# Keeping split mixer weights in DRAM between the two segments of a hybrid decoder block

## The chip, the cores and the metric

One core of a Trainium2 chip runs the whole program. The metric is the device time of one execution in microseconds (us), as the median of several runs. TensorE (PE) does the matrix products, VectorE (DVE) and ScalarE (ACT) the element-wise work, GpSimd (POOL) small copies, and SyncE (SP) issues nearly all DMA transfers. A transfer is spread over up to 16 DMA engines, whichever engine issued it.

## The reference

Input is a sequence of 1024 tokens of width 1024, to which 16 learned meta tokens are prepended (1040 in all). One layer is computed:

```python
h = h + 0.5 * swiglu(rmsnorm(h, ffn1_norm), ffn1_w_gu, ffn1_w_down)      # D_FF 2816
u = rmsnorm(h, mix_norm)
aq, ak, av, az, abeta, aalpha, bcols, ga, gb = split(u @ w_in)           # one input projection
o_a = deltanet(aq, ak, av, az, ...)      # chunked gated DeltaNet, 8 heads of 128
o_b = rwkv7(bcols, ...)                  # RWKV-7 time mixing, 16 heads of 64
h = h + (sigmoid(ga) * o_a + sigmoid(gb) * o_b) @ w_out
h = h + 0.5 * swiglu(rmsnorm(h, ffn2_norm), ffn2_w_gu, ffn2_w_down)
return rmsnorm(h, final_norm)[:, 16:]
```

All arrays are float32, and w_in has, with padding, 75 column tiles of 128.

## The kernel before, in words

The program has three parts one after the other: `ffn1`, `middle` (the two mixers) and `ffn2`. Activations lie transposed, with the model dimension on the 128 partitions and tokens along the free axis.

**Products in two parts.** To keep float32 accuracy at a fast rate of TensorE, every operand of a large product is split into a rounded high part and a low remainder (`split`: ACT writes the high part on L163, DVE the remainder on L164), and three products hi·hi, hi·lo, lo·hi are summed (`mm3`, L307). A weight tile `w` of the mixers therefore has the shape 128 x 2 x 8 x 128: 4 KB per partition for each of the two parts, 1 MB in all, made from a raw tile `wraw` of 512 KB.

**Two segments.** The sequence goes through the mixers in two segments of 528 and 512 tokens (`SEGS`), since the recurrences carry state from one to the other. Each segment needs all 75 column tiles of w_in, so the kernel loads and splits each tile twice: 75 tiles in the first segment, the same 75, in the same roles, in the second. After those come 16 tiles of w_out.

**The order of the weights.** `weight_order` lists every weight tile in the order of its use. `loadw`, called just before a tile's products (in `proj`, whose matmuls write the PSUM tile `pp`), first calls `fetchw` for tiles ahead of the one in use: one tile ahead (`AHEAD = 1`) for w_in. `fetchw` takes a `wraw` tile (two buffers), issues the load from SP's queue (L260), takes a `w` tile (two buffers, `WB = 2`) and splits the one into the other. A buffer comes free when the last instruction that touches it is done.

**The order of the work.** The heads are done in 8 steps per segment. `schedule` says in which order the actions of neighbouring steps are written down: `new_b` and `new_a` project three column tiles each and prepare the operands of a later step, `gates` projects three more, `operands`, `inverses`, `merge_blocks`, `transitions` and `chains` do the recurrences, and `finish` writes one head's result. What is written down earlier has the higher priority; the tool that builds the program orders each engine's instructions by it, taking what it expects to be ready, so the projections' matmuls fill places between the small matmuls of the recurrences. At run time each engine then works strictly in its own fixed order.

**The chain of the inverses.** In each step DVE inverts small triangular blocks (`inverses`: `tb` on L1627, `Xb` on L1629, the copy `Yt` on L1630). The results go through DRAM to be laid out anew, all from SP's queue: `scX` (L1632, twice) and `scY` (L1634, twice) are written, `Xc` (L1637) and `Y` (L1641, four times) are read back. In the first segment `scY` has 51 rows for each of its two transfers, in the second 48. POOL copies a part of `Xc` to `XA` (L1643), and TensorE's first matmul of `merge_blocks` (`iv<-Xc`, L1662) needs `Xc`. Before the inverses, `scr` (L1594, L1597) and `Ub` (L1603) take the blocks to the layout that DVE works on.

**POOL in the mixers.** It does short copies and memsets: `carB` and `carA` (state that the second segment needs), the first columns of `xr` and of the shifted tiles, `XA`, `gam`, `egl`. It issues DMA transfers only at the borders of `middle` (`rdr`, `h2dr`, `h3dr`).

Of the kernel before, what the change touches and what calls it, by code (L numbers as in the profile page):

```python
# [8 lines left out]
F32 = mybir.dt.float32  # L9
F32R = mybir.dt.float32r  # L10
# [3 lines left out]
P = 128  # L14
D = 1024
KD = D // P
# [22 lines left out]
WB = 2  # L39
AHEAD = 1  # L40
# [70 lines left out]
def build(tc, nc, a):  # L111

    ctx = ExitStack()
    with ctx:
        g = K()
        g.tc, g.nc, g.a = tc, nc, a
        nc.scalar.preload_act_table_set("natural_log_exp_and_others")
        pad = ctx.enter_context(tc.tile_pool(name="pad", bufs=1, side="right"))
        nc.vector.memset(pad.tile([P, 24], F32, name="pad"), 0.0)
        const = ctx.enter_context(tc.tile_pool(name="const", bufs=1))  # L120
        wp = ctx.enter_context(tc.tile_pool(name="wp", bufs=2))
        dram = ctx.enter_context(tc.tile_pool(name="dram", bufs=1, space=bass.MemoryType.DRAM))
        g.mmctx = ctx.enter_context(ExitStack())
        main_banks(g, 2, 3, 8)
        g.const, g.wp, g.dram = const, wp, dram

        ones = const.tile([P, P], F32, name="ones")
        nc.vector.memset(ones, 1.0)
        g.pk = const.tile([P, NPK], F32, name="pk")
        nc.sync.dma_start(g.pk, a["pk"])  # L130

        def pv(n):
            o, w = PK[n]
            return g.pk[:, o : o + w]

        nc.vector.tensor_scalar(pv("omu"), pv("mu"), -1.0, 1.0, op0=ALU.mult, op1=ALU.add)
        nc.vector.tensor_scalar(pv("oka"), pv("ka"), -1.0, 1.0, op0=ALU.mult, op1=ALU.add)
        for n in ("w0", "a0"):
            nc.vector.tensor_scalar(pv(n), pv(n), -1.0, None, op0=ALU.mult)
        g.C = lambda n: ones if n == "ones" else g.ck[:, CK[n][0] - P : CK[n][0] - P + CK[n][1]]  # L140
        g.V = lambda n, i=0: g.pk[:, PK[n][0] + i : PK[n][0] + i + 1]

        hdr = [dram.tile([KD, P, sn], F32, name=f"hdr{s}") for s, (_, sn, _) in enumerate(SEGS)]
        mdr = [dram.tile([NJ, P, FULL], F32, name=f"mdr{s}") for s in range(2)]
        g.hdr, g.mdr = hdr, mdr
        g.sdr = dram.tile([NJ, P, P + CB], F32, name="sdr")
        g.gdr = [dram.tile([NJ, FULL], F32, name=f"gdr{s}") for s in range(2)]
        g.rdr = dram.tile([P, FULL], F32, name="rdr")
        g.h2dr = dram.tile([KD, P, FULL], F32, name="h2dr")
        g.h3dr = dram.tile([KD, P, FULL], F32, name="h3dr")  # L150
        g.frm = dram.tile([len(FORMS), HF, P, T // 2], F32, name="frm")

        g.worder, g.wready, g.wfetched, g.wused = list(weight_order()), [], 0, 0
        ffn1(g)
        middle(g)
        ffn2(g)


def split(g, src, hi, lo, eng=None, hi_eng=None):
    if hi_eng:  # L160
        hi_eng.tensor_copy(hi, src)
    else:
        g.nc.scalar.activation(hi, src, AF.Copy)  # L163
    (eng or g.nc.vector).tensor_tensor(lo, src, hi.bitcast(F32), op=ALU.subtract)  # L164
# [6 lines left out]
def schedule():  # L171

    last = 2 * NJ - 1
    yield "segment", 0
    for act in FIRST.split():
        yield act.rstrip("+"), act.count("+")
    for it in range(last + 1):
        order = {NJ - 2: BEFORE_SWITCH, NJ - 1: SWITCH, last - 1: LAST_BUT_ONE, last: FINAL}.get(it, REGULAR)
        for act in order.split():
            if act == "segment":  # L180
                yield act, 1
            else:
                yield act.rstrip("+"), it + act.count("+")
# [11 lines left out]
def weight_order():  # L195

    def down_order(n):
        for r in range(len(FORMS)):
            for m in range(HK):
                for k0, kk in CHUNKS:  # L200
                    yield f"wdn{n}", (r, m, k0), kk

    def tiles(cts, j=0):
        for ct in cts:
            yield "win", (ct + j % NJ,), KD

    yield from down_order(1)
    for act, it in schedule():
        yield from tiles(USES.get(act, ()), 0 if act == "segment" else it)
    for _ in range(2):  # L210
        for m in range(KD):
            yield "wout", (m,), KD

    yield None
    yield from down_order(2)
# [14 lines left out]
def down_weights(g, name, raw, r, m, k0, kk):  # L230

    s = g.wsum[:, m, k0 : k0 + kk]
    if r == 4 and k0 == 0:
        in_turn(g, g.wsum[:, m], block(g, name, m, 0, 0))
    if raw is None:
        return s
    i, j = ((1, 0), (0, 0), (0, 1), None, (1, 0), (0, 1))[r - 1]
    in_turn(g, raw, block(g, name, m, i, j, k0, kk))
    if r == LAST:
        return raw  # L240
    x, y = (raw, s) if r == 3 else (s, raw)
    g.nc.gpsimd.tensor_tensor(s, x, y, op=ALU.add if r == 1 else ALU.subtract)  # L242
    return s


def fetchw(g):
    if not g.worder[g.wfetched]:
        del g.worder[g.wfetched]
    name, idx, kk = g.worder[g.wfetched]
    g.wfetched += 1  # L250
    down = name.startswith("wdn")
    raw = None
    if not down or idx[0] not in (0, 4):
        raw = g.wp.tile([P, KD, P], F32, name="wraw", tag="wraw", bufs=2)[:, :kk]
    if down:
        src = down_weights(g, name, raw, *idx, kk)
        g.wcount += 1
    else:
        src = raw
        g.nc.sync.dma_start(raw, g.a[name][idx])  # L260
    if down and idx[0] == LAST and g.held:
        w = g.held.pop(0)
    elif down and g.wcount % 3 == 0:
        w = g.wthird.tile([P, 2, CHUNKS[0][1], P], F32R, name="w3", tag="w3", bufs=1)
    else:
        w = g.wp.tile([P, 2, KD, P], F32R, name="w", tag="w", bufs=WB)
    split(g, src, w[:, 0, :kk, :], w[:, 1, :kk, :])
    g.wready.append((name, idx, w))


def loadw(g, name, *idx):

    while g.wfetched < len(g.worder) and g.worder[g.wfetched]:
        down = g.worder[g.wfetched][0].startswith("wdn")
        if g.wfetched > g.wused + AHEAD + down or (name == "wdn1" and not down):
            break
        fetchw(g)
    g.wused += 1
    n, i, w = g.wready.pop(0)
    assert (n, i) == (name, idx)  # L280
    return w


def main_banks(g, w, n, banks=6):

    g.mmctx.close()
    g.mmw = w
    pool = lambda name, bufs: g.mmctx.enter_context(
        g.tc.tile_pool(name=name, bufs=bufs, space=bass.MemoryType.PSUM, reuse_waits="tile"))
    g.mm = pool("mm", n)  # L290
    g.mx = pool("mx", banks - n * w)
# [19 lines left out]
class Rms:  # L311


    def __init__(self, g, sq, n, add_on=None):
        self.g, self.sq, self.n, self.acc, self.k = g, sq, n, None, 0
        self.eng = add_on or g.nc.vector
# [331 lines left out]
class Hidden:  # L648
# [15 lines left out]
    def ahead(self):  # L664
        g = self.g
        g.wcount, g.turn, g.held, g.direct = 0, None, [], self.direct
        sums = lambda m: g.nc.sync.dma_start(g.wsum[:, m], block(g, self.name, m, 1, 1))
        self.even += self.places("11", "21")
        self.slots = self.even[:]
        self.load(8, 0)  # L670
        yield
        yield
        sums(0)
        fetchw(g)
        self.split(3)
        yield
        self.even += self.places("t2")
        self.slots = self.even[:HF]
        self.load(HF, 0)
        self.split(6)  # L680
        yield
        sums(1)
        self.split(8)
        yield
        fetchw(g)
        self.split(HF - 1)
        for m in (2, 3):
            sums(m)
        yield
# [31 lines left out]
def down(g, hs, which, n, hidden, hooks):  # L721
# [20 lines left out]
    for r in range(len(FORMS)):  # L742
        cols = halves(n)
        kept = {}
        for m in range(HK):
            hidden.step(r, m)

            def w(k0):
                kept[m, k0] = loadw(g, f"wdn{which}", r, m, k0)
                if k0:  # L750
                    hooks.before(r, m)
                return kept[m, k0]

            product(r, m, (w, w), cols[-1:] if r == LAST else cols)
            hooks.after(r, m, 0)
        if r == LAST and len(cols) > 1:
            for m in range(HK):
                w = lambda k0: kept[m, k0]
                product(r, m, (w, w), cols[:1])
                if m < 2:  # L760
                    fetchw(g)
                hooks.after(r, m, 1)
# [1202 lines left out]
```

## Time and profile before

| | |
|---|---|
| median of 3 runs | 2983.96 us (2981.35 to 2986.49) |
| the profiled execution: its time / its span | 2987.61 us / 2985.8 us |
| mean granted clock of TensorE | 0.990 of full speed |
| first segment of the mixers, projections (about) | 701 to 1480 us |
| second segment, projections (about) | 1480 to 2212 us |
| output projection (about) | 2212 to 2310 us |

The span runs from the first to the last instruction. In rows of the profile, `pp<-uk,w` reads as "writes pp, reads uk and w", `x75` is a count, and what stands in brackets or behind `<-` is the idle time of the engine before the instruction and what ended it. A row by windows gives start and end, the length, then for PE, PEld (TensorE's weight load), DVE, ACT and POOL the busy us and the count, the granted clock, the share of the 16 DMA engines' time and GB/s.

### The profile page before, as it was taken

Reading aid. Unit: us, or ns where it says so; the run is one execution under the profiler, and the core shown is the slowest. Engines: PE = TensorE matmul, PEld = TensorE weight load, DVE = VectorE, ACT = ScalarE, POOL = GpSimd, SP = SyncE. Lnnn points to the kernel's source line nnn. Section 1 sums busy time; section 2 is a strip of 40 time slices with the busy share of each in tenths; the row PEclk is TensorE's granted clock in tenths of the full one; section 3 lists DMA queues with packets and bytes.
Section 4 is the critical chain, followed back from the end, with each engine's and each line's share of the span. In section 5 each row is a group of like instructions: output and inputs, shape, how many; then the busy total and the mean of one; then the engine's idle time right before and its main releaser. Section 6 shows DMA issues by size and latency. Waiting matters only on the chain.

```text
span 2985.8 us, 62816 instructions
## 1 busy us (share of the span) xinstructions
PE 2879.7 (96%) x25584; PEld 2492.5 (83%) x25584; DVE 2209.0 (74%) x4108; ACT 1452.7 (49%) x2554; POOL 498.4 (17%) x576
## 2 busy tenths in 40 slices
PE   8999999999899999999998999999999999999998
PEld 8999999998878888888776777777777888888786
DVE  8666668776767877788877887778876766667886
ACT  6322234345555656565566556656644422223444
POOL 0333233323000000000000000001001032222421
PEclk9999999999989999999999999999999999999999
DMA  3323236553222222333232332233344332333662
GB/s 134 127 105 107 102 121 206 178 195 115 71 69 71 81 71 68 84 81 85 91 96 72 79 85 71 75 88 83 111 138 177 131 107 104 105 104 130 234 220 100
DMA packets 285601, 333.60 MB, mean 112 GB/s; under 512 B 172448, under 2 KB 178720, under 8 KB 285312
## 3 DMA queue, kind: packets, MB, share of 16 engines
q1 hardware_dynamic: 281872, 320.40, 34.5%
q0 software_dynamic: 2000, 6.56, 0.6%
q8 instruction: 201, 3.29, 0.5%
q10 hardware_dynamic: 1440, 2.63, 0.2%
q14 instruction: 88, 0.72, 0.1%
HBM read 261.86 MB, written 67.64 MB: 110 GB/s over the span
## 4 chain that ended last, share of the span: by engine, by line
PE 67%; DVE 19%; ACT 6%; DMA 4%; issue 3%; SPq 1%; POOL 0%; DVEq 0%; ACTq 0%; POOLq 0%
PE pg L513 24%; PE pp L307 16%; PE pd L733 8%; DVE w L164 3%; PE pwo L307 2%; DVE form L164 2%; PE pg L537 1%; DMA form<-frm 1%; DVE tb L1627 1%; DVE Xb L1629 1%; ACT w L163 1%; PE vp L1312 1%; PE mp L1312 1%; PE xp L1312 1%; PE cs L1259 1%
## 5 line engine op out<-in xcount | busy, mean ns | idle before, releaser
L307 PE MATMUL pp<-uk,w 128*128 128x512 f32 (+2 forms) x4824 | 969.6, 347 | 13.5 <-DVE w L164 5.9
L307 PEld LDWEIGHTS pp<-uk,w 128*128 128x128 f32 x4824 | 744.5, 191 | 111.5 <-DVE w L164 14.8
L733 PE MATMUL pd<-form,w 128*128 128x256 f32 (+2 forms) x2772 | 438.6, 320 | 11.1 <-DVE w L164 9.2
L733 PEld LDWEIGHTS pd<-form,w 128*128 128x128 f32 x2772 | 398.1, 190 | 51.1 <-DVE w L164 12.2
L513 PE MATMUL pg<-bt,w 128*128 128x256 f32 (+2 forms) x2520 | 401.7, 318 | 2.5 <-DVE w L164 2.5
L513 PEld LDWEIGHTS pg<-bt,w 128*128 128x128 f32 x2520 | 360.3, 188 | 36.4 <-DVE w L164 3.8
L164 DVE TENSOR_TENSOR w<-wraw,w 128x1024 fp32r<-128x1024 f32 (+2 forms) x266 | 348.4, 1310 | 47.8 <-ACT w L163 45.8
L519 DVE TENSOR_TENSOR c<-c,pg 128x520 f32<-128x520 f32 (+1 forms) x280 | 189.5, 689 | 240.2 <-PE pg L513 216.0
L163 ACT ACTIVATE w<-wraw 128x1024 fp32r<-128x1024 f32 (+2 forms) x266 | 276.3, 1040 | 177.1 <-PE pg L513 115.9
L513 PE MATMUL pg<-b,w 128*128 128x256 f32 (+2 forms) x2160 | 348.1, 317 | 0.0
L513 PEld LDWEIGHTS pg<-b,w 128*128 128x128 f32 x2160 | 309.9, 188 | 28.3 <-DVE w L164 0.3
L163 ACT ACTIVATE w<-wrx 128x1024 fp32r<-128x1024 f32 (+1 forms) x64 | 58.4, 912 | 278.7 <-PE pg L513 239.9
L483 POOL TENSOR_TENSOR wrx<-wrx 128x512 f32<-128x512 f32 x38 | 52.5, 1381 | 612.1 <-DVE w22b L164 435.6
L164 DVE TENSOR_TENSOR form<-form 128x520 fp32r<-128x520 f32 (+1 forms) x152 | 142.2, 971 | 16.2 <-ACT form L163 15.8
L163 ACT ACTIVATE w<-wsum 128x768 fp32r<-128x768 f32 x96 | 75.7, 788 | 156.2 <-PE pd L733 123.1
L164 DVE TENSOR_TENSOR w<-wsum,w 128x768 fp32r<-128x768 f32 x96 | 119.7, 1253 | 34.9 <-ACT w L163 34.9
L163 ACT ACTIVATE form<-form 128x520 fp32r<-128x520 f32 (+1 forms) x152 | 94.2, 632 | 84.4 <-DMA form<-frm 78.5
L1629 DVE TENSOR_TENSOR Xb<-Xb,tb 115x126 f32<-115x126 f32 (+22 forms) x496 | 126.0, 254 | 8.7
L1627 DVE TENSOR_TENSOR tb<-Ub,Xb 115x126 f32<-115x126 f32 (+22 forms) x496 | 125.1, 252 | 8.8 <-DMA Ub<-scr 1.3
L242 POOL TENSOR_TENSOR wsum<-wsum,wraw 128x768 f32<-128x768 f32 (+1 forms) x48 | 94.8, 1988 | 212.4 <-DMA wraw<-in_wdn 211.0
L1436 DVE SCALAR_TENSOR_TENSOR acc<-xr,pk,acc 128x528 f32<-128x528 f32 (+1 forms) x144 | 109.2, 758 | 20.6 <-ACT acc L1432 19.8
L307 PE MATMUL pwo<-uk,w 128*128 128x512 f32 x384 | 96.6, 401 | 1.1 <-DVE uk L164 0.7
(439 smaller groups left out, 4405.0 us busy)
## 6 DMA issues: line engine op xcount, KB each, us to landing
wraw<-in_win SPq DMA_DIRECT2D x150, 512.0 KB
wraw<-in_wgu SPq DMA_DIRECT2D x44, 512.0 KB
wrx<-in_wgu SPq DMA_DIRECT2D x44, 512.0 KB
frm<-c SPq DMA_DIRECT2D x76, 260.0 KB
form<-frm SPq DMA_DIRECT2D x76, 260.0 KB
frm<-c SPq DMA_DIRECT2D x76, 256.0 KB
form<-frm SPq DMA_DIRECT2D x76, 256.0 KB
wraw<-in_wdn SPq DMA_DIRECT2D x40, 384.0 KB
```

Source lines behind the costliest of these rows:

```text
L163: g.nc.scalar.activation(hi, src, AF.Copy)
L164: (eng or g.nc.vector).tensor_tensor(lo, src, hi.bitcast(F32), op=ALU.subtract)
L242: g.nc.gpsimd.tensor_tensor(s, x, y, op=ALU.add if r == 1 else ALU.subtract)
L307: g.last_product = g.nc.tensor.matmul(ps, lhsT=l, rhs=r, start=i == 0, stop=i == n - 1)
L483: sums.tensor_tensor(a22, a21, a22, op=ALU.add)
L513: nc.tensor.matmul(ps[:, c0 : c0 + cn], lhsT=l[:, x, k, :], rhs=r[:, k, y, c0 : c0 + cn], start=i == 0, stop=i == 3 * HK - 1)
L519: nc.vector.tensor_tensor(o, x, y, op=ALU.add)
L733: nc.tensor.matmul(pd[:, c0 : c0 + cn], lhsT=wd[:, u, k - k0, :], rhs=x[:, v, c0 : c0 + cn], start=k + i == 0, stop=k == HF - 1 and i == 2)
L1312: g.nc.tensor.matmul(ps[e][HS[dst], c0 : c0 + CB], lhsT=l, rhs=r, start=True, stop=True)
L1436: nc.vector.scalar_tensor_tensor(acc[:, :n], xr[:, tap : tap + n], V("convw", ct * 4 + tap), acc[:, :n], op0=ALU.mult, op1=ALU.add)
L1627: nc.vector.tensor_tensor(tv, U[:, i, i + 1 :].unsqueeze(2).to_broadcast([npt, nt, ncc]), X[:, i, 0:ncc].unsqueeze(1).to_broadcast([npt, n ...
L1629: nc.vector.tensor_tensor(X[:, i + 1 :, 0:ncc], X[:, i + 1 :, 0:ncc], tv, op=ALU.add)
```

## The change

In the first segment, a tile of w_in that has been split is also written to DRAM as it stands (`wkept`, 1 MB each, 75 of them, in all 78.6 MB), from POOL's queue. `keep` is called in `fetchw` with a lag: the store of a tile is written down when the tile two further on is fetched. In the second segment `fetch_kept` reads the two parts back from SP's queue straight into the place of `w`, without a `wraw` tile and without a split. Since `wraw` isn't needed there, every third tile goes into its two buffers (`Pair`: two loads of 512 KB), so there are three places instead of two, and the fetch runs two tiles ahead instead of one. The test for that looks at the tile's index alone, so it also holds for the w_out tiles with the indices 0 to 7.

```diff
+        g.wkept = [dram.tile([P, 2, KD, P], F32, name=f"wkept{i}") for i in range(75)]
+        g.kept, g.unkept = set(), []
...
+class Pair:
+    def __init__(self, *parts):
+        self.parts = parts
+    def __getitem__(self, at):
+        p, x, k, c = at
+        return self.parts[x][p, k, c]
+
+def keep(g):
+    idx, w = g.unkept.pop(0)
+    g.nc.gpsimd.dma_start(g.wkept[idx[0]], w.bitcast(F32))
+    g.kept.add(idx)
+
+def fetch_kept(g, name, idx):
+    src = g.wkept[idx[0]]
+    g.wcount += 1
+    if g.wcount % 3:
+        w = g.wp.tile([P, 2, KD, P], F32R, name="w", tag="w", bufs=WB)
+        g.nc.sync.dma_start(w.bitcast(F32), src)
+    else:
+        w = Pair(*(g.wp.tile([P, KD, P], F32R, name="wpart", tag="wraw", bufs=2) for _ in range(2)))
+        for x in range(2):
+            g.nc.sync.dma_start(w.parts[x].bitcast(F32), src[:, x])
+    g.wready.append((name, idx, w))
...
 def fetchw(g):
...
     down = name.startswith("wdn")
+    if name == "win" and len(g.unkept) > (idx not in g.kept):
+        keep(g)
+    if idx in g.kept and name == "win":
+        return fetch_kept(g, name, idx)
...
     split(g, src, w[:, 0, :kk, :], w[:, 1, :kk, :])
+    if name == "win":
+        g.unkept.append((idx, w))
     g.wready.append((name, idx, w))
...
 def loadw(g, name, *idx):
...
-        if g.wfetched > g.wused + AHEAD + down or (name == "wdn1" and not down):
+        if g.wfetched > g.wused + AHEAD + (down or g.worder[g.wfetched][1] in g.kept) or (name == "wdn1" and not down):
             break
         fetchw(g)
```

## The prediction

> **What bounds the kernel now.** I read the page's head and its busy times first, then a row for each stage by windows, then what TensorE waited for in the second segment, then the stretches where it waited.
>
> ```profile
> span 2985.8 us, 62816 instructions
> PE 2879.7 (96%) x25584; PEld 2492.5 (83%) x25584; DVE 2209.0 (74%) x4108; ACT 1452.7 (49%) x2554; POOL 498.4 (17%) x576
> ```
>
> ```profile
> 200.00:300.00 100.00, 100.00 (x839) 100.00 (x838) 58.89 (x72) 28.49 (x37) 31.70 (x22) 1.00 0.27 94
> 701.00:1480.00 779.00, 741.77 (x8665) 639.04 (x8663) 583.99 (x1423) 456.09 (x917) 58.29 (x194) 0.98 0.28 77
> 1480.00:2212.00 732.00, 700.98 (x7646) 558.68 (x7647) 585.23 (x1373) 450.85 (x852) 60.04 (x125) 0.99 0.32 85
> 2212.00:2310.00 98.00, 95.02 (x779) 74.67 (x778) 61.41 (x109) 42.33 (x73) 11.48 (x22) 0.98 0.59 193
> ```
>
> TensorE is the bound in every stage. In the second segment, where work is removed, it is busy 700.98 of 732.00 us, so 31.0 us is all the idle time there; DVE, from which most is taken, is busy 80%. Whatever DVE is relieved of, only the part of those 31.0 us that hangs on DVE or ACT can come back, and the time that a low clock costs. Who ended TensorE's waits there:
>
> ```profile
> PE bon L1259 <- ACT hl L163: 9.7, 7, 1.8
> PE pp L307 <- DVE w L164: 4.3, 2, 2.8
> PE np L1312 <- DVE AR L1738: 4.1, 6, 0.8
> PE pp L307 <- ACT acc L1432: 3.0, 1, 3.0
> ```
>
> Three of the longest stand together at 1605 us:
>
> ```profile
> 1605.92 0.73 PE L307 MATMUL pp<-uk,w 128*128 128x512 f32 x2 [2.96 <-ACT acc L1432]
> 1608.21 1.69 PE L1259 MATMUL bon<-hl,bdr 128*128 128x512 f32 x2 [1.56 <-ACT hl L163]
> 1612.73 1.65 PE L307 MATMUL pp<-uk,w 128*128 128x512 f32 x3 [2.82 <-DVE w L164]
> ...
> 1589.84 1.22 DVE L164 TENSOR_TENSOR w<-wraw,w 128x1024 fp32r<-128x1024 f32 x1
> 1611.45 1.22 DVE L164 TENSOR_TENSOR w<-wraw,w 128x1024 fp32r<-128x1024 f32 x1
> ...
> 1604.00:1608.00 4.00, 0.73 (x2) 0.30 (x2) 4.00 (x11) 3.43 (x6) 1.12 (x3) 0.92 0.00 0
> 1608.00:1612.00 4.00, 1.59 (x2) 0.58 (x2) 4.00 (x11) 0.62 (x2) 0.00 (x0) 0.50 0.00 0
> 1612.00:1616.00 4.00, 3.27 (x8) 2.60 (x9) 4.00 (x9) 2.58 (x5) 0.00 (x0) 0.50 0.41 131
> 1616.00:1620.00 4.00, 4.00 (x16) 3.17 (x15) 2.06 (x5) 0.11 (x1) 0.00 (x0) 0.80 0.74 160
> ```
>
> There DVE is busy without a gap (4.00 of 4.00 us in three rows), TensorE waits 7.34 us in all, and its clock is then granted at half: 0.64 + 4 + 4 + 1.6 = 10.2 us at half, in which it is busy about 6.5 us (1.59 + 3.27 + 1.6), work of 3.2 us at full clock. So the three waits cost 7.3 + 3.2 us.
>
> **What is removed: 75 loads of 512 KB and 75 splits in the second segment.** All splits of the mixers' tiles in this window:
>
> ```profile
> L164 DVE TENSOR_TENSOR w<-wraw,w 128x1024 fp32r<-128x1024 f32 x77 | 94.5, 1227 | 5.6 <-ACT w L163 5.1
> L163 ACT ACTIVATE w<-wraw 128x1024 fp32r<-128x1024 f32 x75 | 79.0, 1054 | 2.8 <-PE pp L307 2.5
> ```
>
> 75 x 1.227 = 92 us leave DVE and 79 us leave ACT; DVE falls from 80% to 67% of the window. Nearly all of it lay beside TensorE's work. What returns, by place. At 1605: the wait of 2.82 us for a split goes; of the other 4.52 us the two DVE splits in the busy stretch before them (2 x 1.22 = 2.4 us) go; the low clock goes with it, 3.2 us. That is 8.4 us. Elsewhere the wait for w is 4.3 - 2.8 = 1.5 us, all of it. The waits for `bon` are 9.7 - 1.56 = 8.1 us in six places; ACT's `hl` comes behind DVE's chain of `new_b`, in which splits are mixed: I take half, 4.0 us (bounds 0 and 8.1). The waits for `np` end with one DVE instruction behind others: a third of 4.1, 1.4 us. The gain is 8.4 + 1.5 + 4.0 + 1.4 = 15.3 us. Its bounds: 4.3 us (the waits for w alone) and 31.0 + 3.2 = 34 us.
>
> **What is added in the second segment: loads of 1 MB from SP's queue.** Their price in engine time: the first stage moves large rows at 94 GB/s in 0.27 of the engines' time, 348 GB/s at full use, so 1 MB takes 3.0 us and 512 KB 1.5 us. Landing, by the nearest row of a large transfer:
>
> ```profile
> L930 POOL DMA_DIRECT2D h3dr<-hh x8: 539/540/544, 2285.9 to 2327.0; - x8
> DMA to landing us min/median/max: 2.3/2.4/9.1
> ...
> 1480.13 21.67 PE pp L307 x94
> ```
>
> 256 KB from POOL's queue land in 2.4 us; 768 KB more at 348 GB/s add 2.3, so 4.7 us is the lower bound, and four times 2.4 = 9.6 us the upper; I take 4.7, since these rows move large packets too. With three places, a tile's load starts when TensorE is done with the tile three before it, and two tiles lie between: 24 matmuls x 21.67 / 94 = 5.5 us each, 11.1 us. Both bounds fit: nothing, while cover lasts; without it 5 us at each run of six projections. SP now waits for TensorE at these loads instead of for DVE; behind it stand the transfers of the inverses' chain, which are needed later than the tile waited for. The 25 further issues of the pairs lie on SP, which ends none of the four waits above. The one tile more of prefetch at w_out: nothing, at most the 3.0 us idle of its window.
>
> **What is added in the first segment: 75 stores of 1 MB from POOL.** Issue: 0.54 us each by the row above, 2.2 us if it grew with size; 41 to 162 us on an engine that is busy 58.29 of 779 us. I take nothing. The store waits for DVE's remainder; queued behind it on POOL are `carB`, `carA`, `XA` and `gam`, and TensorE waits for `XA` alone; the upper end is 2.2 us in each of 8 steps, 18 us.
>
> The store also holds the `w` place: the split of the tile two further on must wait until it has landed. The tightest regular place:
>
> ```profile
> 1007.40 1.22 DVE L164 TENSOR_TENSOR w<-wraw,w 128x1024 fp32r<-128x1024 f32 x1
> ...
> 1016.42 1.06 ACT L163 ACTIVATE w<-wraw 128x1024 fp32r<-128x1024 f32 x1
> ```
>
> The first ends a tile at 1008.62, the second begins the next tile in the same place: 7.8 us of room for 0.54 + 4.7 = 5.2 us. Nothing; at the upper landing 10.1 us it is 2.3 us late, once in each of 8 steps, 18 us.
>
> **Where I see the cost: the inverses' chain.** 75 x 3.0 us more put the engines' share from 0.28 to 0.57 in this segment, and two stores fall on each step's chain:
>
> ```profile
> 1017.64 1.22 DVE L164 TENSOR_TENSOR w<-wraw,w 128x1024 fp32r<-128x1024 f32 x1
> 1024.86 1.22 DVE L164 TENSOR_TENSOR w<-wraw,w 128x1024 fp32r<-128x1024 f32 x1
> ...
> 1019.79 2.45 SPq L1632 DMA_DIRECT2D scX<-Xb  x2
> 1026.67 2.98 SPq L1637 DMA_DIRECT2D Xc<-scX  x1
> ...
> 1032.53 1.39 POOL L1643 COPY XA<-Xc 32x128 f32<-32x128 f32 x2 [3.13 <-DMA Xc<-scX]
> 1034.24 0.75 PE L1662 MATMUL iv<-Xc,LT 32*32 32x32 f32 x32
> ...
> 1408.53 2.01 POOL L1643 COPY XA<-Xc 32x128 f32<-32x128 f32 x2 [2.51 <-DMA Xc<-scX]
> 1410.86 0.75 PE L1662 MATMUL iv<-Xc,LT 32*32 32x32 f32 x32
> ...
> 851.80 0.75 PE L1662 MATMUL iv<-Xc,LT 32*32 32x32 f32 x32 [1.33 <-DMA Xc<-scX]
> ...
> 1785.34 0.97 POOL L1643 COPY XA<-Xc 32x128 f32<-32x128 f32 x2 [1.42 <-DMA Xc<-scX]
> 1794.59 0.75 PE L1662 MATMUL iv<-Xc,LT 32*32 32x32 f32 x32
> ```
>
> Tiles are ready at 1018.86 and 1026.08, so their stores move just as `scX` and then `Xc` do. `Xc` has landed when POOL starts on it (1032.53) and TensorE needs it at 1034.24: 1.7 us of slack, 2.3 at 1408 (the first and last of five alike), none at 851, where TensorE already waited 1.33. The delay of the chain is between 0 and 6.0 us (both stores wholly in front). No row shows a POOL store beside this chain; I take the middle, 3.0. TensorE then waits 3.0 - 2.0 = 1.0 us in five steps and 3.0 in the first: 8.0 us (bounds 0 and 4.0 x 5 + 6.0 = 26). In the second segment the slack is 9.3 us (1785 to 1794), so the larger loads there cost nothing.
>
> On this point the Trainium skill, "DMA: Bandwidth & Descriptors", section "Issuing engines are not separate DMA queues", says that transfers of all issuing engines run on the same 16 engines and interleave. No row here tests it on this chain. Were POOL's transfers apart, the 8.0 us would be none and the sum would give 2969; by the rule it stands.
>
> **The sum.** -15.3 + 8.0 = -7.3 us against the profiled execution, whose span is 2985.8 and whose time is 2987.61 us, 0.12% over the median of the runs, 2983.96. The difference is set against the median: 2977.
>
> **The rivals.** *No change.* The relief is hidden as nearly all DVE work is: TensorE's waits move to the next late producer in the fixed orders, the gain is 4.3 to 11 us, and the stores give it back: 2978 to 2990. For it: TensorE's 96%, and gaps spread over many places. Against it: the one place at 1605, where DVE is plainly late. *Slower, by the chain.* The chain's delay is the whole 6.0 us: 26 us of waits, each of 4.0 us or more. At 1605 waits of 2.96, 1.56 and 2.82 us brought half clock worth 3.2 us; at half of that for each of six waits, 9.6 us more. 26 + 9.6 - 15.3 = +20, 3004. It decides from the delay d at which 5 (d - 2.0) + d = 15.3: 4.2 us. For it: the stores fall on the chain by the rows. Against it: the chain shares engines with a 512 KB load already. Here a page speaks too: the Trainium skill, "TensorE: Matmul & The Clock Gate", section "Why this matters for your kernels", warns of idle gaps over about 3 us between matmul bursts. The rows at 1605 agree (half clock after gaps of up to 2.96 us). *Slower, by the places.* Landing nearer to 9.6 us makes splits or the copies behind POOL's issues late, 18 us: 18 + 8.0 - 15.3 = +11, 2995. Against it: 0.54 us an issue.
>
> **How the numbers follow.** Less than 0.2% (6.0 us) can hardly be told from no change here. Forecast, faster: 0.42, with 2962 to 2978 as its own range (its upper half of the gain, 34 less a cost of 12, to the bound). No change: 0.27. Slower: 0.31, of it 0.21 by the chain and 0.10 by the places. The range that leaves out 2 in 10 runs from 2960 (most of the 34 us, cost near none) to 3006 (the chain's case).
>
> **What would show it.** In the second segment the splits are gone from DVE and ACT, its busy share is near 67%, and the three waits at 1605 with their half clock shrink. In the first, `iv<-Xc` waits for DMA in most steps by about 1 us, DMA's share is near 0.57, and ACT's splits never wait for a store. The prediction is wrong if `iv<-Xc` waits 4 us a step, if `pp` waits for DMA in the second segment, or if the `bon` waits stay as they are.

## The result, and the profile after

| | before | after |
|---|---|---|
| median time, us | 2985.05 | 3020.12 |
| ratio to before (95% interval) | 1 | 1.0131 (1.0113 to 1.0148) |
| profiled span, us | 2985.8 | 3018.1 |
| mean granted clock | 0.990 | 0.983 |

The change costs 35 us by the two medians and 39 us by the ratio; a gain of 7 was forecast. Of all runs below, one counts as slow and stands in no ratio: 5425 us, one of seven executions of the change with the shorter chain. The page's head and busy times after:

```profile
span 3018.1 us, 62920 instructions
PE 2896.5 (96%) x25584; PEld 2510.8 (83%) x25584; DVE 2126.9 (70%) x4033; ACT 1391.3 (46%) x2479; POOL 513.4 (17%) x651
```

The 75 splits are gone: DVE has 75 instructions and 82 us less than before, ACT 75 and 61 us. TensorE does the same 25584 matmuls, but is busy 17 us longer. Where the time went is seen when the span is cut by work instead of by the clock on the wall: at the first projection, the first `iv<-Xc` of the first step, that of the seventh step, the first matmul of w_out, and its last. In the rows by windows, first of before, then of after, the columns are start and end, length, then busy us and count of PE, PEld, DVE, ACT and POOL, the granted clock, the DMA share and GB/s:

```profile
701.00:851.00 150.00, 133.46 (x1183) 120.81 (x1181) 106.48 (x220) 95.84 (x174) 21.79 (x56) 0.99 0.27 79
851.00:1411.00 560.00, 542.35 (x6646) 467.65 (x6648) 423.59 (x1063) 320.54 (x659) 35.12 (x132) 0.98 0.28 75
1411.00:2210.00 799.00, 764.94 (x8481) 607.62 (x8478) 637.15 (x1508) 488.60 (x934) 61.42 (x131) 0.99 0.31 85
2210.00:2326.00 116.00, 113.02 (x858) 89.56 (x857) 74.91 (x129) 50.50 (x83) 13.10 (x25) 0.99 0.58 190
```

```profile
699.00:865.00 166.00, 139.98 (x1177) 126.53 (x1175) 105.70 (x219) 95.56 (x173) 29.55 (x73) 0.92 0.55 179
865.00:1461.00 596.00, 555.30 (x6638) 477.89 (x6638) 424.64 (x1064) 323.11 (x662) 55.63 (x180) 0.96 0.51 157
1461.00:2252.00 791.00, 766.65 (x8480) 611.63 (x8481) 561.92 (x1443) 423.33 (x854) 45.23 (x139) 0.99 0.48 144
2252.00:2364.00 112.00, 110.81 (x860) 89.05 (x859) 73.12 (x116) 50.96 (x85) 13.02 (x25) 1.00 0.60 197
```

The matmul counts of each pair agree within 0.6%, so these are the same stretches of work. The first segment loses 16 and 36 us, 52 in all. For the same matmuls TensorE is busy 19.5 us longer (6.5 + 13.0), at a clock of 0.92 and 0.96 in place of 0.99 and 0.98, and idle 32.5 us longer (26.0 - 16.5 in the first row, 40.7 - 17.7 in the second). The second segment and w_out give 8 + 4 us back. That is 40 us; the stretches of ffn1 and ffn2 at both ends, which the change doesn't touch, were 8 us shorter in this execution, so the spans differ by 32.3 us. What TensorE waited for, first in the first segment, then in the second:

```profile
PE iv L1702 <- DMA Xc<-scX: 23.3, 7, 8.6
PE bon L1299 <- ACT hl L165: 6.7, 7, 2.2
```

```profile
PE np L1352 <- DVE AR L1778: 5.6, 8, 0.8
PE iv L1710 <- ACT T L1705: 3.8, 1, 3.8
PE pp L347 <- DMA wpart<-wkept: 3.0, 1, 3.0
...
PE bon L1299 <- ACT hl L165: 0.2, 1, 0.2
```

In the first segment the inverses' chain has become late in seven of its eight steps, 23.3 us in place of 1.3 (8.6 in the first step, 1.5 to 3.3 in each of the next six; the eighth has no store beside it). In the second, the waits for `bon` (9.7 us before) and for splits (4.3 us) are gone but for 0.2 us, and two waits have come where the segments meet: 3.0 us for a stored tile at 1540 and 3.8 us for ACT at 1564, each with a stretch of low clock behind it. The chain itself, in the step whose rows of before stand in the prediction, by the timeline after:

```profile
1038.69 1.23 DVE L166 TENSOR_TENSOR w<-wraw,w 128x1024 fp32r<-128x1024 f32 x1 [1.23 <-ACT w L165]
1040.21 0.53 POOL L262 DMA_DIRECT2D wkept<-w  x1 [4.43 <-DVE tb L1667]
1040.85 3.82 SPq L1672 DMA_DIRECT2D scX<-Xb  x2
1045.04 5.61 SPq L1674 DMA_DIRECT2D scY<-Yt  x2
1047.41 0.53 POOL L262 DMA_DIRECT2D wkept<-w  x1 [2.73 <-DVE w L166]
1050.83 5.09 SPq L1677 DMA_DIRECT2D Xc<-scX  x1
1058.73 0.75 PE L1702 MATMUL iv<-Xc,LT 32*32 32x32 f32 x32 [1.90 <-DMA Xc<-scX]
```

and the one row of before that the prediction doesn't have:

```profile
1022.62 3.88 SPq L1634 DMA_DIRECT2D scY<-Yt  x2
```

One store goes out 0.6 us ahead of `scX`, one while SP is still issuing `scY`. From the start of `scX` to the end of `Xc`'s row the chain took 9.86 us before (1019.79 to 1029.65) and takes 15.07 us now: 5.2 us late, with 2 us of slack. In the other steps POOL's copy of `Xc` stands 4.7 to 5.8 us further behind `scX` than before, and 8.3 us in the first, where three stores go out beside the chain. In the step shown TensorE waits only 1.90 us, since it reaches this place later itself: but for the wait it would be there 15.98 us after the start of `scX`, and before it was after 14.45 us.

### The profile page after: what moved, and what is told of

It reads as the page before. It is cut to its first block, busy times and chain, and to the rows that moved or that the text cites. A ratio compares the mean times of both kernels' runs of the same rounds, so it can differ in the third digit from the quotient of the medians.

```text
span 3018.1 us, 62920 instructions
## 1 busy us (share of the span) xinstructions
PE 2896.5 (96%) x25584; PEld 2510.8 (83%) x25584; DVE 2126.9 (70%) x4033; ACT 1391.3 (46%) x2479; POOL 513.4 (17%) x651
## 4 chain that ended last, share of the span: by engine, by line
PE 70%; DVE 12%; DMA 7%; ACT 5%; issue 5%; SPq 1%; POOL 1%; DVEq 0%; POOLq 0%; ACTq 0%
PE pg L553 24%; PE pp L347 19%; PE pd L773 10%; DMA Xc<-scX 2%; DVE w L166 2%; PE pg L577 1%; PE cs L1299 1%; PE xp L1352 1%; PE pwo L347 1%; PE vp L1352 1%; ACT w L165 1%; DMA wkept<-w 1%; DMA form<-frm 1%; PE gra L1553 1%; DMA Ub<-scr 1%
## 5 line engine op out<-in xcount | busy, mean ns | idle before, releaser
L347 PE MATMUL pp<-uk,w 128*128 128x512 f32 (+2 forms) x4224 | 832.0, 343 | 5.5 <-ACT w L165 2.0
L347 PEld LDWEIGHTS pp<-uk,w 128*128 128x128 f32 x4224 | 648.5, 195 | 77.9 <-issue 6.3
L166 DVE TENSOR_TENSOR w<-wraw,w 128x1024 fp32r<-128x1024 f32 (+2 forms) x191 | 256.3, 1342 | 48.6 <-ACT w L165 47.4
L165 ACT ACTIVATE w<-wraw 128x1024 fp32r<-128x1024 f32 (+2 forms) x191 | 197.5, 1034 | 177.7 <-PE pg L553 115.8
L347 PE MATMUL pp<-uk,wpart 128*128 128x512 f32 x600 | 154.4, 402 | 3.0 <-DMA wpart<-wkept 3.0
L347 PEld LDWEIGHTS pp<-uk,wpart 128*128 128x128 f32 x600 | 113.0, 192 | 27.6 <-DMA wpart<-wkept 3.5
L165 ACT ACTIVATE form<-form 128x520 fp32r<-128x520 f32 (+1 forms) x152 | 94.6, 632 | 81.5 <-DMA form<-frm 79.8
```

The costliest lines, as they stand in the source:

```text
L347: g.last_product = g.nc.tensor.matmul(ps, lhsT=l, rhs=r, start=i == 0, stop=i == n - 1)
```

## The experiments

Two theories stood against each other and the order of work as a third. *Place*: a store delays the chain when it is issued beside it, by the whole time that it takes on the DMA engines. *Bytes, or POOL*: each store costs something wherever it stands. *Order*: the loss comes from the second segment's three buffers and the other order of work there.

**The stores alone, and the read-back alone.** In the first kernel the second segment no longer asks for kept tiles, and it fetches one tile ahead, as before the change:

```diff
-    if idx in g.kept and name == "win":
-        return fetch_kept(g, name, idx)
...
```

> The 75 stores are kept, the second segment loads and splits its tiles as before the change. Theory: the stores run on the DMA engines in front of the inverses' chain, 5 us late in each step, and the waits with their half clock cost the first segment about 48 us (the six steps from 939 to 1411 took 472 us before and 505 us after, the stretch ahead of them 238 and 257). So 2985 + 48 = 3033 (3020 to 3040). Rival, the order: the loss comes from the second segment's three buffers and the other order of work there; then the stores alone cost under 10 us, 2985 to 2995.

In the second only three tiles are stored, and all loads of the second segment read those, so that its projections work with wrong weights and only the time counts:

```diff
...
-    src = g.wkept[idx[0]]
+    src = g.wkept[LORA[idx[0] % 3]]
...
```

> Only three tiles are stored, at the start, and every load of the second segment reads one of these three: the loads of 1 MB, the three buffers and the missing splits are as in the change, 72 stores are gone (the projections there work with wrong weights). Theory: the read-back alone gains what the prediction said, 11 us (six steps 1.9 us shorter each) to 20 us: 2965 to 2974. Rival, the order: the second segment is no better in itself, 2985 or slower, and the switch between the segments costs.

Measured: the stores alone 1.0163 (1.0150 to 1.0176), some 48 us slower; the read-back alone 0.9947 (0.9933 to 0.9961), some 16 us faster. (Each ratio is against runs of before on the same chip, with medians of 2980 to 2981 us.) Together they give 1.011, which agrees with the whole change's 1.0113 to 1.0148 when their own intervals are counted in. The loss belongs to the stores and the gain to the read-back; the order as the cause is out. The four steps from the third `iv<-Xc` to the seventh by windows, of before, of the stores alone and of the read-back alone:

```profile
1034.20:1410.90 376.70, 366.12 (x4507) 315.24 (x4508) 290.86 (x723) 224.48 (x460) 24.44 (x88) 1.00 0.29 76
```

```profile
1059.20:1457.60 398.40, 374.23 (x4506) 321.40 (x4506) 290.96 (x722) 224.65 (x459) 39.47 (x124) 0.98 0.53 167
```

```profile
1030.50:1407.70 377.20, 366.05 (x4505) 315.16 (x4504) 290.81 (x723) 224.29 (x460) 24.54 (x88) 1.00 0.29 76
```

94.2 us a step before, 99.6 with the stores, 94.3 with the read-back alone.

**Fewer stores, by place.** Of the stores alone, without the 15 beside the chain, and then those 15 alone:

```diff
+NOT_KEPT = {59, 67, 50, *range(2, 8), *range(18, 24)}
...
-    if name == "win" and idx not in g.seen:
+    if name == "win" and idx not in g.seen and idx[0] not in NOT_KEPT:
```

> Stores alone, as in the run with all 75, but without the 15 that were issued from 1 us before to 12 us after scX in the steps of the first segment (tiles 59, 67, 50, 2 to 7, 18 to 23); the other 60 MB are stored as there. Theory: what costs is the place on the chain, not the bytes: the steps fall from 99.7 to 94.5 us, the first step's chain from 20 to 13 us; 3028 - 6 x 5.3 - 10 = 2986 (2983 to 2996). Rival, bytes or POOL's queue: a fifth of the stores is gone, and with it a fifth of the 47 us: 3019.

> Stores alone, but only the 15 that were issued from 1 us before to 12 us after scX in the first segment's steps (tiles 59, 67, 50, 2 to 7, 18 to 23); the other 60 are left out. Theory: these 15 carry what the other 60 do not (47 - 18 = 29 us): 2981 + 29 = 3010 (3003 to 3020), with the chain at 17 us a step. Rival, bytes: a fifth of the stores costs a fifth, 9 us: 2990.

Measured: without the 15, 1.0063 (1.0050 to 1.0076), 19 us slower; the 15 alone, 1.0123 (1.0099 to 1.0147), 37 us slower. The same four steps, without the 15 and with only the 15:

```profile
1038.00:1419.50 381.50, 367.89 (x4505) 316.74 (x4504) 291.22 (x723) 224.47 (x460) 38.68 (x117) 1.00 0.49 152
```

```profile
1054.30:1450.40 396.10, 373.09 (x4506) 321.01 (x4507) 290.39 (x722) 224.56 (x459) 24.50 (x96) 0.98 0.34 93
```

and what TensorE waited for in the first segment with only the 15:

```profile
PE iv L1702 <- DMA Xc<-scX: 25.5, 7, 8.7
```

This is the plainest pair. With a DMA share of 0.49 but nothing beside the chain, a step takes 95.4 us and TensorE has no wait for `Xc` in these steps (1.4 us in the first step, as before); with a share of 0.34 and two stores on the chain it takes 99.0 us, and the waits are 25.5 us, as with all 75. So the place makes the larger part. It doesn't make all: the other 60 still cost 19 us (15 to 23) where the theory said 5. By the profiles, 10.7 us apart, 7.3 of them arise in two steps (939.22 to 1128.60 us before, 939.55 to 1136.25 here): TensorE waits 4.0 us for `bon` in place of 1.0, at a clock of 0.98 in place of 1.00. The three steps behind them cost 1 us in all. What set it off in these two steps is the hold of the place: ACT's split waits there for the landing of the store that holds its place, 3.0 us in two waits, 1.65 us of it in the first (at 1020.39). DVE's part of the split, the inverses' last instructions and `hl` for `bon` come as much later, and TensorE waits 2.12 us for `bon` (at 1028.80) where it waited 0.51 before. With only the 15 stores the splits wait 0.7 us in all and `bon` 3.6 us in the first segment (3.9 before). That 19 + 37 is more than 48 lies within the intervals.

**Half of each store.**

```diff
...
-    g.nc.gpsimd.dma_start(g.wkept[idx[0]], w.bitcast(F32))
+    g.nc.gpsimd.dma_start(g.wkept[idx[0]], w[:, 1].bitcast(F32))
...
```

> Stores alone, all 75, but of the second half of each tile, 512 KB. Theory: a store stands in the chain's way for as long as the engines move it, 1.5 us each instead of 3.0: the chain is 2.6 us late instead of 5.2, slack 2.0: TensorE waits 0.6 us a step and the half clock mostly goes; 2990 (2985 to 3000). Rival, a fixed price for each store (its issue on POOL, its place): the time stays at 3020 to 3028.

Measured: 1.0025 (1.0012 to 1.0037), 7 us slower. The four steps, and the wait:

```profile
1038.10:1417.30 379.20, 366.70 (x4504) 315.25 (x4504) 290.52 (x722) 224.22 (x460) 40.32 (x124) 1.00 0.44 125
```

```profile
PE iv L1701 <- DMA Xc<-scX: 7.0, 5, 5.8
```

As many issues on POOL as with whole stores, and a sixth of the loss: a fixed price for each store is out. Half the delay (POOL's copy is 1.8 to 3.1 us later than before in six steps) nearly fits into the slack of 2 us, so the loss falls by far more than half. 5.8 of the remaining 7.0 us are the first step's, which has no slack. A half store lands in 5.2 us in place of 6.6; no split of ACT waits for one, and the waits for `bon` are 3.4 us, less than before.

**A shorter chain.** In the first segment `scY` is written as 48 rows, like in the second, and its last three rows behind `Xc`; with the change, with the stores alone, and without either:

```diff
-        nc.sync.dma_start(scY[:nblk, :, r, :], Yt[64 * r : 64 * r + nblk])
+        nc.sync.dma_start(scY[:NBLK, :, r, :], Yt[64 * r : 64 * r + NBLK])
...
+        for r in range(2):
+            nc.sync.dma_start(scY[NBLK:, :, r, :], Yt[64 * r + NBLK : 64 * r + nblk])
```

> The change as it is, but in the first segment scY is written as 48 rows, like in the second segment, and its last three rows by transfers of their own behind Xc. Theory: 51 rows run on about 3 of the 16 engines (about 260 packets of 128 B a microsecond for 6 us, where the read of the same data moves over 900), and the second store shares those; with 48 rows scY takes some 2 us, the chain is 4 us shorter, the 5 us of delay become about 1 us, less than the 2 us of slack, and the waits of TensorE for Xc (23 us) and the half clock after them go: 3020 - 45 = 2975 (2968 to 2985). Rival, bandwidth: 75 MB of stores cost whatever stands beside them, and the time stays at 3010 to 3020.

> The kernel before with the same rewriting of scY and nothing else. Theory: the chain has 2 us of slack there, so a shorter chain is worth only the 1.3 us wait of the first step and the low clock behind it: 2975 to 2985. Rival: TensorE's order itself hangs on the chain, and 4 us come back in each of 7 steps: 2957.

> All 75 stores, no read-back, scY as 48 rows. Theory: the rewriting takes 29 us off the whole change (3020 to 2991), and it acts in the first segment only, so it takes as much off the stores alone: 3028 - 29 = 2999 (2992 to 3008). Rival: part of the 29 us lies where the read-back begins; then 3010 or slower here.

Measured: with the change 1.0031 (1.0019 to 1.0043), with the stores alone 1.0101 (1.0077 to 1.0124), without either 0.9997 (0.9987 to 1.0007). A chain of the first kernel, by the timeline of SP:

```profile
1129.61 4.24 SPq L1672 DMA_DIRECT2D scX<-Xb  x2
1133.91 2.90 SPq L1674 DMA_DIRECT2D scY<-Yt  x2
1138.18 0.38 SPq L1677 DMA_DIRECT2D Xc<-scX  x1
```

and its two stores by that of POOL:

```profile
1129.45 0.53 POOL L262 DMA_DIRECT2D wkept<-w  x1 [3.37 <-DVE Xb L1669]
1137.04 0.54 POOL L262 DMA_DIRECT2D wkept<-w  x1 [3.89 <-issue]
1144.15 0.99 POOL L1683 COPY XA<-Xc 32x128 f32<-32x128 f32 x2 [4.49 <-DMA Xc<-scX]
```

`scY` goes out in 2.9 us in place of 5.6, and the change is 30 us faster with it, while the waits for `Xc` in the first segment fall from 23.3 to 6.3 us: they, and the low clock behind them, were the larger part of the loss. But `Xc`, issued 1.1 us behind the second store, is copied only at 1144.15, 5.6 us after the end of its issue; in the kernel before that was 2.9 us (1029.65 to 1032.53). From the start of `scX` to this copy it is 14.5 us, against 7.9 in the same step of the rewriting without stores, so the delay is not the 1 us expected; the shorter chain only bears it (TensorE doesn't wait in this step). Of the 6.3 us that are left 5.7 stand in the first two steps. These waits alone don't make up the 19 us by which the seventh step's `iv<-Xc` is still later than before; where the rest comes from, and why the expected 2975 was not reached, stays open. With the stores alone the rewriting brought 18 us by the medians and not the 29 expected; by the profiles the first segment gained 30 us in both (the seventh step's `iv<-Xc` starts at 1428.0 in place of 1457.6, and 1429.8 in place of 1461.1), and with the stores alone the rest of the run, in another order, took 7 us more (1583.6 in place of 1576.8).

**Versions that might beat both kernels.** The change with 48 rows and without the 15 stores; with only the second half of each tile stored, and the first half made again by ACT:

> The change without the 15 stores on the chain (their tiles are loaded and split in the second segment as before the change), and scY as 48 rows. Theory: the first segment is that of the kernel with three stored tiles (steps 94.1 us), the second keeps four fifths of the gain, 13 of 16 us: 2981 - 13 + 3 for the start = 2971 (2963 to 2978). Rival: the mixed order of split and stored tiles in the second segment brings back waits for w, 2980 to 2990.

> Only the second half of each split tile is stored (512 KB); the second segment loads the weights and this half and makes the first half again on ScalarE, with two buffers as before the change; scY as 48 rows. Theory: the delay of 2.6 us is within the slack, so the first segment costs some 3 us at its start, and VectorE's 92 us of splits are gone from the second: of the 16 us most hang on VectorE: 2981 + 3 - 11 = 2973 (2966 to 2982). Rival: the gain of the second segment comes from the third buffer and from ScalarE; then 2980 to 2987.

Measured: 1.0125 (1.0110 to 1.0141) and 1.0095 (1.0082 to 1.0108), both far from what was expected. In the first segment the four steps from the third `iv<-Xc` on came out near the expectation (94.6 and 95.3 us each), but the seventh step's `iv<-Xc` is 13 and 9 us later than before, where 3 were expected; the second segment missed it by more. Two of the first kernel's steps there by windows, and the longest wait of the second kernel there:

```profile
1811.10:1913.80 102.70, 99.30 (x994) 78.99 (x994) 73.98 (x173) 56.13 (x109) 7.16 (x18) 0.97 0.44 132
1913.80:1986.90 73.10, 71.58 (x892) 57.73 (x893) 53.56 (x147) 38.50 (x81) 3.41 (x13) 1.00 0.37 105
```

```profile
PE pp L343 <- ACT w L272: 13.9, 9, 2.9
```

In the first kernel the tiles split anew and the pairs want the same two `wraw` places, and the steps are uneven; in the second, with two buffers, TensorE waits for ACT. That raised the question what the third buffer is worth. The read-back alone (again with wrong weights), with two buffers and one tile ahead:

```diff
...
-    g.wcount += 1
-    if g.wcount % 3:
-        ...
-    else:
-        w = Pair(...)
+    w = g.wp.tile([P, 2, KD, P], F32R, name="w", tag="w", bufs=WB)
+    g.nc.sync.dma_start(w.bitcast(F32), src)
```

> The kernel with three stored tiles whose second segment reads only these (its projections there work with wrong weights), but with two buffers and a prefetch of one tile, as before the change, instead of three and two. Theory, relief: the gain of 16 us comes from the splits that leave VectorE and ScalarE, the place of the third buffer is hidden; 2965 (2960 to 2970). Rival, the buffers: with two places a load of 1 MB starts only when the tile two before it is done, one tile of cover (5.5 us) against a landing of 4.7 to 9.6 us, so TensorE waits for w in each run of six projections, and the gain is gone: 2980 or slower. A kernel that reads half of each tile and makes the other half with two buffers waited 13.9 us for it.

Measured: 1.0072 (1.0049 to 1.0094), 21 us slower than before, against 16 us faster with three. Its longest wait in the second segment:

```profile
PE pp L343 <- DMA w<-wkept: 17.3, 7, 4.2
```

So the third buffer, with the fetch of one tile more that it allows, is worth some 37 us: without it the loads of 1 MB come late, and the rival holds. Then the change without the 15 stores with two buffers, where two raw tiles in nine give the loads more room, once with 48 rows and once without; and two that leave out only early stores:

> The change without the 15 stores on the chain and with scY as 48 rows, with two buffers in the second segment. The same with three buffers has a first segment of 94.3 us a step, but steps of 103, 73 and 92 us in turn in the second, because split and stored tiles share the raw tiles' places. Theory: without the pairs in those places the steps there are even, 86 us: 3019 - 3 x 7 - 10 = 2975 to 2985. Rival, the buffers: waits for loads of 1 MB, 3000 or slower.

> The change without the 15 stores on the chain, two buffers and a prefetch of one tile in the second segment, scY as it was. Theory: the first segment is that of the run with the other 60 stores alone (9 us slower than before at its last step), the second that of the same kernel with 48 rows (85.3 us a step in place of 86.9, and 9 us at its start): 2981 + 9 - 16 = 2974 (2968 to 2982). Rival: the even steps came from the other order that the rewriting of scY brought; then waits for the loads of 1 MB as in the run with two buffers, 2990 to 3010.

> The change with scY as 48 rows, without the six stores that stand near the chain of the first two steps (tiles 24, 59, 67, 50, 2, 18), three buffers in the second segment. Theory: of the 28 us between the change with 48 rows and the kernel with three stored tiles, 23 arise ahead of the third step; half of them go: 2991 - 12 = 2979 (2972 to 2986). Rival: the six tiles that are split again upset the pairs' places at the start of the second segment and the low clock returns, 2990 to 3000.

> The change with scY as 48 rows, where the first 24 tiles of the order are not stored, so that the stores begin at the third step; the second segment splits these 24 and reads back the other 51 in one run. Theory: the first segment up to the third step is as before the change (23 us back), the steps from there cost 1 us each, and the second segment gains only from its fourth step on, 1.9 us a step: 2981 + 5 - 10 = 2976 (2970 to 2985). Rival: the busy place at 1605, where the splits stay, holds the gain; 2985.

Measured, in this order: 1.0012 (0.9997 to 1.0027), 1.0034 (1.0018 to 1.0049), 1.0021 (1.0009 to 1.0034), 1.0014 (1.0002 to 1.0027). The uneven steps are gone in the first of them:

```profile
1816.00:1901.50 85.50, 83.70 (x942) 67.19 (x941) 63.47 (x160) 47.43 (x96) 5.36 (x15) 1.00 0.43 126
1901.50:1987.30 85.80, 83.82 (x943) 67.24 (x944) 63.44 (x160) 47.41 (x96) 5.36 (x15) 1.00 0.43 126
```

and so they are without the 48 rows (85.2 us), against the rival of that run; that its median is nevertheless 17 us over the expectation, with a profiled span of 2985.1, stays open. All four are near the kernel before, and none beats it. By the profiles they lose 4.5 to 17 us up to the seventh step's `iv<-Xc` and gain 9 to 13 us behind it, so what the first segment loses uses up the gain of the second; how much of that loss is the remaining stores, and how much another order of work, the runs don't part. Only the read-back without the stores is clearly faster, and with its wrong weights it is no version of the kernel.

## Why the prediction was wrong

**The steps that failed are the size of the chain's delay, and two costs in the first segment that were put at nothing: the low clock, and the hold of the place by stores away from the chain.** The prediction had the place (two stores on `scX` and `Xc` in each step), the slack (2 us), the bounds (0 and 6.0 us) and the point from which it decides (4.2 us). It then took the middle, 3.0 us, because no row showed a store beside this chain. The measured delay is 5.2 us, near the whole time that the engines take for two stores. With it the prediction's own sum is (5.2 - 2.0) x 5 + 5.2 = 21.2 us of waits where 8.0 stand; measured are 23.3 us, 1.3 of them old. That these agree so well is in part luck: the sum leaves out the second step (2.3 us), the other six waits are 2.5 us on average and not 3.2, and the first is 8.6. The middle was no evidence. The rows had a hint: at 1018.88 a load of `wraw` goes out 0.9 us ahead of `scX`, so the chain already stood behind a large transfer of every step, and its 12 us from `Yt` to `XA` held that. The prediction used this load as a reason against a delay.

**The first step** was given the same delay as the others. There three stores fall on the chain, not two, and its single wait for `Xc` is 8.6 us.

**The low clock was priced at nothing in the forecast.** The rival "slower, by the chain" had it, with 9.6 us; measured are 19.5 us of longer busy time for the same matmuls. This rival, 3004, is what happened, in place, kind and sign; its 26 us of waits were near (23.3), its clock too cheap by half, and the range's upper end of 3006 hung on it.

**The hold of the place** was put at nothing too, since 5.2 us fit into 7.8 us of room. Stores land in 6.7 us by the page after (the median, up to 10.3), not in the 4.7 assumed, and in two steps that is too late. The first of the two, by the timeline after:

```profile
1037.59 1.06 ACT L165 ACTIVATE w<-wraw 128x1024 fp32r<-128x1024 f32 x1 [1.32 <-DMA wkept<-w]
1046.01 0.56 PE L1299 MATMUL bon<-hl,bdr 128*128 128x512 f32 x1 [1.80 <-ACT hl L165]
```

In the next step the pair is 1.74 and 2.22 us. The waits of the splits are few, four with 4.2 us in all, but the chain behind them ends at TensorE and brings the low clock. This is the rival "slower, by the places" in a smaller form, and a part of the 19 us that the 60 stores cost. In the profile after, of the 52 us that the first segment loses, 22.0 are new waits for `Xc` and 19.5 longer busy time; the other 10.5 us are idle time that the forecast doesn't have, 2.8 of it more for `bon`.

**The gain was right in sum, by parts that erred both ways.** 15.3 us were forecast for the second segment; the read-back alone gave 16 (interval 12 to 20), the rows of the whole change 8 and, at w_out, 4, where at most 3.0 were expected. The parts: at 1605 the waits and the low clock are gone, as said. The waits for `bon` went almost wholly (9.7 to 0.2 us), not by half. The waits for `np` did not shrink (4.1 to 5.6 us). One reading was wrong: of the two splits said to lie ahead of the first two waits at 1605, the second (1611.45) starts after both have ended and is the one that the third wait, of 2.82 us, is for, so 1.2 us were counted twice.

**The cover of three places was right, and more important than said.** The loads of 1 MB were set at nothing while 11 us of cover last, and at 5 us for each run of projections without; the third place is worth 37 us. One wait of 3.0 us came where the segments meet, at 1540, 8 us after the last store was issued.

**POOL's issue was rightly nothing.** Each issue took 0.53 us, and the half stores, with as many issues, cost 7 us in all. Of the listed signs, `iv<-Xc` waits for DMA in most steps, but by 2.5 us on average in those behind the first, and not 1; the DMA share came out at 0.51 to 0.55 (0.57 forecast), and DVE in the second segment at 561.92 of 791 us, 71% (67%).

On the rule that all issuing engines share the 16 DMA engines (the Trainium skill, "DMA: Bandwidth & Descriptors", section "Issuing engines are not separate DMA queues"): the runs agree, since POOL's stores delay SP's small transfers by about their whole time. The rule alone gives no size; "interleave" reads as a half share, and 5.2 of 6.0 us is nearly all of it.

Open: what the 60 stores away from the chain cost beyond these two steps, and whether the delay arises in the engines or in SP's issue, whose rows grew as well (`scX` from 2.45 to 3.82 us).

## What to carry to other kernels

Before transfers are added to a quiet stretch, list the chains of small dependent transfers there, and count against each chain's slack the whole engine time of every large transfer issued beside it, not a share; here 5.2 of 6.0 us came through. A chain with some 2 us of slack bore two stores of 512 KB almost without a wait, and not two of 1 MB. A store also holds the buffer that it reads until it has landed: count its longest landing, not the shortest, against the next use of the buffer. And where a load takes the place of a computation, the gain may hang on one more buffer than the computation needed: try it alone first.

## What the runs showed of the hardware

**Waits under 2 us can halve the clock.** In the step shown above the two longest waits are 1.80 us (for `bon`, at 1046.01) and 1.90 us (for `Xc`, at 1058.73). Windows of after around them:

```profile
1044.00:1048.00 4.00, 2.20 (x11) 1.93 (x10) 4.00 (x9) 1.19 (x2) 1.05 (x3) 0.79 1.12 262
1048.00:1052.00 4.00, 4.00 (x28) 3.90 (x27) 2.04 (x5) 0.97 (x2) 0.22 (x2) 0.78 0.80 251
...
1056.00:1060.00 4.00, 2.10 (x53) 1.77 (x52) 1.58 (x3) 2.73 (x5) 1.11 (x4) 1.00 0.81 189
1060.00:1064.00 4.00, 4.00 (x17) 3.23 (x16) 0.78 (x2) 2.19 (x5) 0.90 (x4) 0.58 0.98 312
```

Behind each, the clock is at half for some 3.4 us (0.79 and 0.78 of two windows of 4 us, 0.58 of one). TensorE was busy about half of the 4 us around each wait (2.20 and 2.10 us), and the idle time of each is that one wait. Another place of this trace tells one long gap from a share of idle time: from 701.6 to 705.0 us TensorE is busy 1.93 of 3.40 us, with two shorter waits of 0.83 and 0.64 us, and the clock granted from 705.0 to 708.5 is 0.52. So it is rather the share of idle time in some 3.4 us than one long gap. The warning that the Trainium skill gives on idle gaps of over about 3 us ("TensorE: Matmul & The Clock Gate", "Why this matters for your kernels") doesn't cover these.

**51 rows move far more slowly than 48.** While `scY` moved with 51 rows, in the kernel before, the engines' share was 0.26:

```profile
1024.00:1028.00 4.00, 3.49 (x27) 3.19 (x27) 4.00 (x7) 0.63 (x1) 0.00 (x0) 1.00 0.26 39
```

With 48 rows, in the rewriting without the change, it was 0.80 from 1016 to 1020 us, and SP's row of `scY` in this step took 1.61 us in place of 3.88. (Such a row alone is no measure: in the second segment of the kernel before, behind two loads, 48 rows took 3.90 us.) The Trainium skill has a rule that fits ("DMA: Bandwidth & Descriptors", "Why a DMA increments its semaphore by 16 and not by 1"): a transfer uses the largest number of engines up to 16 that divides the size of the slowest dimension on both sides, 3 for 51 rows and 16 for 48. The shares and the shorter chain with 48 rows agree; no view here shows the number of engines itself.
